# One encoder layer on one core: the weight ring moves to the upper end of the memory, and the moving operands of scores, up and down projection to its lower half

## The chip, the core and the metric

The kernel runs on one core of a Trainium2 chip. The metric is the time of one execution in microseconds of device time. Of the engines that the texts name, TensorE (PE in the profile) multiplies matrices, VectorE (DVE) and ScalarE (ACT) work elementwise, GpSimd (POOL) does little here, and SyncE (SP) issues the transfers. A matmul holds a 128x128 block still in the array (the stationary operand) and passes the other one through (the moving operand, 128, 256 or 512 columns here).

## What is computed

```python
u  = rmsnorm(x, norm1_g)
hq, hi, hf_f, hf_b, hgate, aq, ak, av, ga, gb = split(u @ w_in)
o_a = hgrn2_bidirectional(hq, hi, hf_f, hf_b, hgate, ...)   # gated linear recurrence, 4 heads
o_b = gqa_bidirectional(aq, ak, av, ...)                    # rotary attention, 8 heads on 2 kv heads
merged = sigmoid(ga) * (o_a @ w_branch_a) + sigmoid(gb) * (o_b @ w_branch_b)
x  = x + merged @ w_out
up = dwconv_centred(rmsnorm(x, norm2_g) @ w_up, conv_w, conv_b)
val, gate = split(up)
x  = x + (silu(gate) * val) @ w_down
```

All arrays are fp32; x is 1024 x 1024, w_in 1024 x 5376 in ten parts, w_up 1024 x 5632, w_down 2816 x 1024.

## The kernel before

Every fp32 operand of a large product is split into a high part (a cast to fp32r on ACT, L77) and a low part (the difference, on DVE, L78), and every product is three matmuls: high by high, high by low, low by high (`mm3`, L91 to L94; `gate_steps`, L276; `product`, L761). A list `name_h`, `name_l`, or one tile with both halves, holds the two parts.

The stages follow one another on PE, with work of the next stage mixed in by a scheduler of the framework, which sets the order of instructions on each engine from the program and from priorities (`tc.high_priority`):

- The first norm and transposition of x into `uT` (four tiles of 16 KiB a partition), and the products `vg`, `hp`, `v`, `sg` of the recurrence, with the recurrence itself. In `hp` and in the gate products `gp` (L276) `uT` moves, 512 columns at a time; in `v`, `sg` and later `rk`, `rq` (`gemm_t`) `uT` is stationary and 256 columns of weight move.
- Attention: `scores` (L567, L568) with `qT` stationary and `kT` moving, 512 columns; `turn` transposes the probabilities; `values` (L598) with `vv` stationary and the transposed probabilities moving, 256 columns. Gate products fill the gaps (`fill`).
- The two branch products `y` (weights stationary, branch outputs `oah`, `oal`, `ob`, `obh`, `obl` moving) and `wo` (`mT` stationary, the split w_out moving).
- The up projection as seven products (`m1` to `m7`) for each of 22 blocks j. Weight blocks are stationary; the moving operands are `c0b` and `c1t` (in the pool `cp`) and `xt3`, `xt4`, `xb22` (in the pool `xr`), all 512 columns. `hidden` applies the convolution and the gate and writes the left operands of the down projection to `left_d`.
- The down projection as seven products of eleven steps each (`down`). A step n = 0, 1, 2, ... loads a left block (`left`), splits it and a block of w_down (or a sum of two) into `dz`, and does twelve matmuls into four banks: four of L92, then pairs of L93 and L94. In the first product the banks are called `da`.

Memory is handed out by pools. Pools without `side` are put one above the other from the bottom of a partition, those with `side="right"` one below the other from the top, and each keeps its place until it is closed. The offsets in this text are bytes of a partition, counted up from the pools' sizes. Before, `const` ends at 19,584; `wpool` (the ring `wp` of three 8-KiB slots, and two `raw` buffers of 4 KiB) lies at 19,584 to 52,352; `uT`, and after it the tiles of `cp`, at 52,352 to 117,888; then the small gate buffers. At the right, `kT` and `vv`, later `ob0`, `ob1`, `wo00`, `wo02`, `wo03`, lie at 172,000 to 196,576 (`apk`), and `xt3`, `xt4`, `xb22` between 133,088 and 182,240 (`xr`). `dz` is a tile of the ring.

The loads of w_down into the blocks `W[0][k]` (L968) and of the left blocks (L979) go through SP's queue, as do the stores of `hidden` into `left_d` (L898, L907). Before, the blocks of w_down have places in `c0w` (8 halves), `c1w` (16 halves) and ten tiles `w`; left blocks 0 to 7 have places in `c0left`, 8 to 10 in `raw` buffers, and from step 11 on they come through a ring of four tiles `dr`. L1024 is a difference of two blocks of w_down, which a later product needs.

Of the kernel before, what the change touches and what calls it, by code (L numbers as in the profile page):

```python
# [17 lines left out]
P = 128  # L18
# [26 lines left out]
def hybrid_kernel(ctx: ExitStack, tc: tile.TileContext, x, gn, vec, cst, rope,  # L45
# [10 lines left out]
    wpool = pool("wpool", 2, wst)  # L56
# [85 lines left out]
    mid = ExitStack()  # L142
    upool = pool("upool", 1, mid)
    uT = [tuple(upool.tile([P, KT, 512], F32R, name=f"uT{i}{n}") for n in "hl") for i in range(2)]

    gstp = pool("gstp", 2, mid)
# [29 lines left out]
    def gate_silu(sg, u):  # L176
        for i in range(2):
# [16 lines left out]
          [wide(np_.tile([P, 2 * L], F32R, name=f"vg1{n}", bufs=1)) for n in "hl"]]  # L194

    def wide_block(i, n):
        raw = wpool.tile([P, L], F32, tag="raw", name=f"raw_vg{i}{n}")
        nc.sync.dma_start(raw, win_t[2 * n + i])
        split(vg[i][0][:, :, n, :], vg[i][1][:, :, n, :], raw.rearrange("p (k c) -> p k c", k=4))

    def wide_gemm(t):
        ps = gps.tile([P, 512], F32, tag="g", name=f"vg_{t}")
        h, l = uT[t // 4]
        o = slice((t % 4) * P, (t % 4 + 1) * P)
        for k in range(KT):
            bh, bl = (z[:, k % 4].rearrange("p n c -> p (n c)") for z in vg[k // 4])
            end = mm3(ps, h[:, k, o], l[:, k, o], bh, bl, k == 0, k == KT - 1)
        S.copy(vts[0][:, t, :], ps[:, 0:256])
        V.tensor_copy(sg[:, t, :], ps[:, 256:512])
        return end  # L210
# [57 lines left out]
    def gate_steps(c):  # L268
        wh, wl = weight_block(win_f[12 + c], f"g{c}")
        for half in range(2):  # L270
            ps = gps.tile([P, 512], F32, tag="g", name=f"gp{c}{half}")
            h, l = uT[half]
            for k in range(KT):
                w = slice(k * P, (k + 1) * P)
                for n, (a, b) in enumerate(((wh, h), (wh, l), (wl, h))):
                    yield T.matmul(ps, a[:, w], b[:, k, :], start=k == 0 and n == 0, stop=k == KT - 1 and n == 2)  # L276
            gt = gstp.tile([P, 512], F32, tag="gt", name=f"gt{c}{half}")
            S.copy(gt, ps)
            nc.sync.dma_start(gate_d[c, :, half * 512:(half + 1) * 512], gt)
# [159 lines left out]
    apk = pool("apk", 1, kst, side="right")  # L439
# [187 lines left out]
    mid.close()  # L627


    cst_ = ExitStack()  # L630
    cp = pool("cp", 2, cst_)
    xs2 = lambda t: cp.tile([P, D], F32, tag="xs", name=f"xs2{t}", bufs=1)
    cols = lambda tag, name: tuple(cp.tile([P, KT, 512], F32R, tag=tag, name=f"{name}{n}") for n in "hl")
# [78 lines left out]
    def normed_columns(t):  # L712
        nc.sync.dma_start(h_d[t], acc[t])
        xs = normed(xs2(t), acc[t], gb2, f"b{t}")
# [62 lines left out]
    def prep_sums(j):  # L777
        r1 = r1s.pop(j)
        r2 = cp.tile([P, 2, NH], F32, tag="xs", name=f"r2_{j}", bufs=1) if j else two(slot_v("r2_0", F32)[0])
# [42 lines left out]
    a22 = cp.tile([P, 2, NH], F32, tag="xs", name="a22_0", bufs=1)[:, 1]  # L822
# [20 lines left out]

    xr = pool("xr", 1, ust, side="right")
    xr_tile = lambda tag, j, shape, dt=F32, n=1: xr.tile(shape, dt, tag=tag, name=f"{tag}_{j}", bufs=n)
    split_4(0, a22)
    for nm in ("t3", "t4", "b22"):
        xop[nm] = tuple(xr.tile([P, 4, NH], F32R, name=f"x{nm}{n}") for n in "hl")
# [106 lines left out]
    wq, early = eight("c0w"), eight("c0left")  # L955
    early = [early[:, i] for i in range(KT)]
    for i in range(2):
        r = wpool.tile([P, 2, NH], F32, tag="raw", name=f"left{i}")
        early += [r[:, 0], r[:, 1]]
    where = [wq[:, 2 * i:2 * i + 2] for i in range(4)]  # L960
    for wq in (eight("c1w0"), eight("c1w1")):
        where += [wq[:, 2 * i:2 * i + 2] for i in range(4)]
    where += [dl_.tile([P, 2, NH], F32, tag="w", name=f"w{i}", bufs=10) for i in range(10)]
# [8 lines left out]
    def down(ps, i, first, right, load=None, after=None):  # L972

        for k in range(NK):
            n = next(nstep)
            raw = dl_.tile([P, 2, NH], F32, tag="raw", name=f"dr{n}", bufs=4) if n >= NK else None
# [5 lines left out]
            z = [y.rearrange("p (n c) -> p n c", n=2) for y in halves(ring(f"dz{n}"))]  # L982
# [154 lines left out]
```

## Time and profile before

| | before |
|---|---|
| time, median of 3 runs (lowest to highest) | 1601.61 us (1598.26 to 1604.12) |
| profiled execution: its own time | 1601.28 us |
| profiled execution: span, first to last instruction | 1599.2 us |
| mean granted TensorE clock | 0.997 |
| PE busy | 1567.0 us (98%), 8056 matmuls |
| weight loads (PEld) busy, beside PE | 1309.5 us (82%) |
| DVE busy | 1113.4 us (70%) |
| ACT busy | 771.0 us (48%) |
| POOL busy | 35.1 us (2%) |

The span is 2.1 us shorter than the profiled execution's own time. Busy times are sums over all instructions of an engine. Matmuls are pipelined: one that is listed with 0.39 us starts some 0.23 us after the one ahead of it, so the distance of two starts, and not the duration, is what a matmul takes of PE's time.

### The profile page before, as it was taken

What the parts mean: (1) busy time and instruction counts of PE and PEld (TensorE: products, weight loads), DVE (VectorE), ACT (ScalarE), POOL (GpSimd) and SP (SyncE); (2) the same over time, 40 slices, a digit from 0 to 9 for tenths busy, and PEclk for the clock granted to TensorE, in tenths of its full rate; (3) what the DMA queues carried; (4) which work ended last, traced back from release to release, by engine and by line L of the source; (5) the groups of instructions that cost most, each with busy time, mean ns of one, the idle gap of its engine ahead of it and who ended that gap; (6) DMA issues with size and microseconds to landing.
All of it is one profiled execution on the core that took longest, in us unless ns stands there. A gap on an engine that the chain in (4) does not pass through costs nothing.

```text
span 1599.2 us, 20536 instructions
## 1 busy us (share of the span) xinstructions
PE 1567.0 (98%) x8056; PEld 1309.5 (82%) x8056; DVE 1113.4 (70%) x1648; ACT 771.0 (48%) x1205; POOL 35.1 (2%) x33
## 2 busy tenths in 40 slices
PE   8999999999999999999999989999999999999998
PEld 6889998889988888887888867788788788787887
DVE  5367566545768888887653387787888787967586
ACT  5276354524556566666432344444544444544432
POOL 0000000000000000000000061000000000000000
PEclk9999999999999999999999999999999999999999
DMA  5011111222010101012444112322232234685333
GB/s 205 27 40 40 53 40 53 81 77 80 27 60 27 47 32 42 27 47 106 154 151 179 57 46 66 106 102 96 99 99 99 101 111 139 223 308 185 100 119 105
DMA packets 59761, 150.29 MB, mean 94 GB/s; under 512 B 6161, under 2 KB 6417, under 8 KB 59666
## 3 DMA queue, kind: packets, MB, share of 16 engines
q1 hardware_dynamic: 59666, 148.99, 27.6%
q8 instruction: 63, 1.03, 0.3%
q14 instruction: 32, 0.26, 0.1%
HBM read 109.91 MB, written 39.06 MB: 93 GB/s over the span
## 4 chain that ended last, share of the span: by engine, by line
PE 83%; DVE 7%; DMA 4%; ACT 4%; issue 1%; SPq 1%; DVEq 0%; ACTq 0%
PE pa L761 13%; PE gp L276 10%; PE pc L761 6%; PE pt L587 4%; PE pv L598 4%; PE pb L761 3%; PE s L567 2%; PE y L92 2%; PE y L94 2%; PE y L93 2%; PE hp L93 2%; PE hp L94 2%; PE hp L92 2%; PE s L568 2%; PE wo L94 2%; PE wo L93 2%
## 5 line engine op out<-in xcount | busy, mean ns | idle before, releaser
L77 ACT CAST pth<-pt 128x512 fp32r<-128x512 f32 x128 | 71.2, 588 | 59.2 <-PE pt L587 58.9
L77 ACT CAST dz<-dr 128x512 fp32r<-128x512 f32 (+1 forms) x66 | 50.6, 767 | 101.8 <-PE da L94 35.8
L78 DVE TENSOR_TENSOR dz<-dr,dz 128x512 fp32r<-128x512 f32 (+1 forms) x66 | 56.9, 867 | 50.5 <-ACT dz L77 50.2
L573 ACT ACTIVATE p<-s,m 128x1024 f32<-128x1024 f32 x64 | 71.9, 1123 | 34.1 <-DVE m L570 34.1
L276 PE MATMUL gp<-uT1h,w_g 128*128 128x512 f32 x256 | 86.1, 397 | 0.0
L276 PE MATMUL gp<-uT0h,w_g 128*128 128x512 f32 x256 | 86.0, 396 | 0.0
L78 DVE TENSOR_TENSOR ptl<-pt,pth 128x512 fp32r<-128x512 f32 x128 | 82.4, 681 | 4.6 <-ACT pth L77 4.6
L570 DVE TENSOR_REDUCE m<-s 128x1 f32<-128x1024 f32 x64 | 78.1, 1220 | 6.2 <-PE s L568 4.4
L761 PE MATMUL pc<-c1t,wb 128*128 128x512 f32 x264 | 69.5, 398 | 5.4 <-ACT c1t L77 5.0
L761 PE MATMUL pa<-c0b,wa 128*128 128x512 f32 x264 | 69.1, 394 | 4.0 <-ACT wa L77 2.9
L587 PEld LDWEIGHTS pt<-cs,p 128*128 128x128 f32 x512 | 56.4, 140 | 19.9 <-DVE ptl L78 9.5
L587 PE MATMUL pt<-cs,p 128*128 128x128 f32 x512 | 71.0, 277 | 1.6 <-DVE p L575 0.9
L761 PE MATMUL pb<-c0b,wa 128*128 128x512 f32 x264 | 68.7, 391 | 0.5 <-DVE ta L734 0.5
L761 PE MATMUL pa<-c1t,wb 128*128 128x512 f32 x264 | 67.5, 393 | 0.0
L598 PE MATMUL pv<-pth,vv 128*128 128x256 f32 x256 | 65.2, 293 | 0.0
L77 ACT CAST wc<-r 128x1024 fp32r<-128x1024 f32 x22 | 23.1, 1052 | 86.3 <-PE pc L761 76.5
L761 PEld LDWEIGHTS pc<-c1t,wb 128*128 128x128 f32 x264 | 50.5, 192 | 17.0 <-ACT c1t L77 5.2
L761 PEld LDWEIGHTS pa<-c0b,wa 128*128 128x128 f32 x264 | 48.9, 188 | 17.5 <-ACT wa L77 5.6
L598 PE MATMUL pv<-ptl,vv 128*128 128x256 f32 x256 | 62.6, 282 | 0.4 <-DVE ptl L78 0.4
L761 PEld LDWEIGHTS pa<-c1t,wb 128*128 128x128 f32 x264 | 49.8, 189 | 12.0 <-DVE c1t L78 0.4
L761 PEld LDWEIGHTS pb<-c0b,wa 128*128 128x128 f32 x264 | 49.5, 188 | 11.5 <-DVE ta L734 0.9
L888 DVE SCALAR_TENSOR_TENSOR cv<-c,vc,cv 128x1023 f32<-128x1023 f32 x44 | 56.2, 1278 | 2.5 <-ACT cv L887 2.5
(461 smaller groups left out, 4467.4 us busy)
## 6 DMA issues: line engine op xcount, KB each, us to landing
r<-in_wup_dram SPq DMA_DIRECT2D x44, 512.0 KB, 3.4
left_d<-cv SPq DMA_DIRECT2D x33, 512.0 KB, 3.2
dr<-left_d SPq DMA_DIRECT2D x66, 256.0 KB, 2.7
raw_g<-in_win_f_dram SPq DMA_DIRECT2D x16, 512.0 KB, 3.4
gate_d<-gt SPq DMA_DIRECT2D x32, 256.0 KB, 2.0
gl<-gate_d SPq DMA_DIRECT2D x16, 512.0 KB, 4.0
raw_h<-in_win_f_dram SPq DMA_DIRECT2D x12, 512.0 KB, 3.4
w<-in_wdown_dram SPq DMA_DIRECT2D x20, 256.0 KB, 5.4
```

The source lines that it names most:

```text
L77: S.copy(h, src)
L78: V.tensor_tensor(out=l, in0=src, in1=h.bitcast(F32), op=ALU.subtract)
L92: T.matmul(ps, ah, bh, start=first, stop=False, skip_group_check=more)
L93: T.matmul(ps, ah, bl, start=False, stop=False, skip_group_check=more)
L94: return T.matmul(ps, al, bh, start=False, stop=last, skip_group_check=more)
L276: yield T.matmul(ps, a[:, w], b[:, k, :], start=k == 0 and n == 0, stop=k == KT - 1 and n == 2)
L570: V.tensor_reduce(out=m, in_=s, axis=AX.X, op=ALU.max, negate=True)
L573: S.activation(pb, s, AF.Exp, bias=m, accum_out=z)
L587: pin(T.transpose(pt[:, i, :], pb[:, k * P:(k + 1) * P], ident))
L598: pin(T.matmul(pv, vv[pair // 2][:, k, :], pts[u][k // 4][n][:, k % 4, :, :], start=k == 0 and n == 0, stop=k == KT - 1 and n == 1))
L761: T.matmul(ps, a[:, k * P:(k + 1) * P], x[:, k, :], start=first and n == 0, stop=n == len(seq) - 1, skip_group_check=not first)
L888: V.scalar_tensor_tensor(out=cv[:, 1:], in0=src[:, :-1], scalar=w0, in1=cv[:, 1:], op0=ALU.mult, op1=ALU.add)
```

## The change

The pools change places, and some tiles change pools; no product, split or transfer of the large arrays is left out. `wpool` opens on the right side and lies at 192,480 to 225,248, with one row buffer `xs` of 4 KiB above it. `cp` opens at the start, at 19,584 to 85,120, and `uT` lives in its tiles. `apk` (`kT`, `vv`, `ob0`, `ob1`, `wo00`, `wo02`, `wo03`, `r2_0`) opens on the left, at 85,120 to 109,696. `xt3`, `xt4`, `xb22` get a pool of their own on the left, `xl`, at 85,120 to 134,272 (`xb22h` from 117,888 to 126,080, `xb22l` above it). What used the gate buffers and `cp`'s tag `xs` uses the row buffer. `vg1` is split in four halves of 4 KiB, with two more casts and two more differences. In the down projection `dz` has three fixed places in `c0dz` and `c0left`; the left blocks 0 to 3 lie in the rest of `c0left`, 4 to 9 in the `raw` buffers and the row buffer, and step 10 is the first that loads through `dr`. The blocks of w_down lie in `c1w` (16 halves), in the three tiles of the ring (`w`) and in eight tiles `wd`; the early places `c0w` are gone.

```diff
-    wpool = pool("wpool", 2, wst)
+    wpool = pool("wpool", 2, wst, side="right")
...
-    mid = ExitStack()
-    upool = pool("upool", 1, mid)
-    uT = [tuple(upool.tile([P, KT, 512], F32R, name=f"uT{i}{n}") for n in "hl") for i in range(2)]
-
-    gstp = pool("gstp", 2, mid)
+
+    cst_ = ExitStack()
+    cp = pool("cp", 2, cst_)
+    row = lambda name: wpool.tile([P, D], F32, tag="xs", name=name, bufs=1)
+    cols = lambda tag, name: tuple(cp.tile([P, KT, 512], F32R, tag=tag, name=f"{name}{n}") for n in "hl")
+    uT = [cols(f"c{i}", f"uT{i}") for i in range(2)]
...
-          [wide(np_.tile([P, 2 * L], F32R, name=f"vg1{n}", bufs=1)) for n in "hl"]]
+          [[hp2.tile([P, L], F32R, tag="k", name=f"vg1{n}{i}", bufs=4).rearrange("p (k n c) -> p k n c", k=2, n=2)
+            for i in range(2)] for n in "hl"]]
...
+        gt = row(f"gt{c}")
...
-            gt = gstp.tile([P, 512], F32, tag="gt", name=f"gt{c}{half}")
-            S.copy(gt, ps)
-            nc.sync.dma_start(gate_d[c, :, half * 512:(half + 1) * 512], gt)
+            w = slice(half * 512, (half + 1) * 512)
+            S.copy(gt[:, w], ps)
+            nc.sync.dma_start(gate_d[c, :, w], gt[:, w])
...
-    apk = pool("apk", 1, kst, side="right")
+    apk = pool("apk", 1, kst)
...
-        xs = normed(xs2(t), acc[t], gb2, f"b{t}")
+        xs = normed(row(f"xs2{t}"), acc[t], gb2, f"b{t}")
...
-        r2 = cp.tile([P, 2, NH], F32, tag="xs", name=f"r2_{j}", bufs=1) if j else two(slot_v("r2_0", F32)[0])
+        r2 = two(row(f"r2_{j}")) if j else two(slot_v("r2_0", F32)[0])
...
+    xl = pool("xl", 1, ust)
     xr = pool("xr", 1, ust, side="right")
...
-        xop[nm] = tuple(xr.tile([P, 4, NH], F32R, name=f"x{nm}{n}") for n in "hl")
+        xop[nm] = tuple(xl.tile([P, 4, NH], F32R, name=f"x{nm}{n}") for n in "hl")
...
-    wq, early = eight("c0w"), eight("c0left")
-    early = [early[:, i] for i in range(KT)]
+    za, zb = cp.tile([P, 2, 2, L], F32R, tag="c0", name="c0dz"), cp.tile([P, 2, 2, L], F32R, tag="c0", name="c0left")
+    dz = [za[:, 0], za[:, 1], zb[:, 0]]
+    early = [zb[:, 1, i // 2, (i % 2) * NH:(i % 2 + 1) * NH].bitcast(F32) for i in range(4)]
     for i in range(2):
-        r = wpool.tile([P, 2, NH], F32, tag="raw", name=f"left{i}")
+        r = two(wpool.tile([P, L], F32, tag="raw", name=f"left{i}"))
         early += [r[:, 0], r[:, 1]]
-    where = [wq[:, 2 * i:2 * i + 2] for i in range(4)]
+    r = two(row("left2"))
+    early += [r[:, 0], r[:, 1]]
+    where = []
...
-    where += [dl_.tile([P, 2, NH], F32, tag="w", name=f"w{i}", bufs=10) for i in range(10)]
+    for i in range(3):
+        wq = ring(f"w{i}", F32)
+        where += [two(wq[:, n]) for n in range(2)]
+    where += [dl_.tile([P, 2, NH], F32, tag="w", name=f"wd{i}", bufs=8) for i in range(8)]
...
-            raw = dl_.tile([P, 2, NH], F32, tag="raw", name=f"dr{n}", bufs=4) if n >= NK else None
+            raw = dl_.tile([P, 2, NH], F32, tag="raw", name=f"dr{n}", bufs=4) if n >= len(early) else None
...
-            z = [y.rearrange("p (n c) -> p n c", n=2) for y in halves(ring(f"dz{n}"))]
+            z = [y.rearrange("p (n c) -> p n c", n=2) for y in halves(dz[n % 3])]
```

The order of instructions changes most where the up projection ends and the down projection begins. The line numbers of the changed kernel are up to eleven higher there: L878, L886, L893, L894, L909, L917, L918, L920, L921, L990 and L1035 answer to L873, L881, L888, L889, L904, L912, L913, L915, L916, L979 and L1024.

On DVE before, around the splits of step 2 of the down projection (`dz_11649`; `dz_11668` is step 3):

```order
L78 TENSOR_TENSOR dz_11649<-c0left,dz_11649 128x512
L1024 TENSOR_TENSOR c1w_11598<-c1w_11598 128x512
L889 SCALAR_TENSOR_TENSOR cv_11491<-c_10_11324,vc,cv_11491 128x1023
L78 TENSOR_TENSOR dz_11649<-c0w,dz_11649 128x512
L1024 TENSOR_TENSOR c1w_11597<-c1w_11597 128x512 x3
L915 TENSOR_TENSOR cv_11355<-cv_11355,cv_11224 128x512
L888 SCALAR_TENSOR_TENSOR cv_11567<-c_21_11539,vc,cv_11567 128x1023
L904 TENSOR_TENSOR cv_11487<-cv_11487,cv_11491 128x1024
L881 TENSOR_TENSOR c_21_11456<-pc_11512,u_21_11510 128x512
L78 TENSOR_TENSOR dz_11668<-c0left,dz_11668 128x512
L916 TENSOR_TENSOR cv_11355<-cv_11355 128x512
L78 TENSOR_TENSOR dz_11668<-c0w,dz_11668 128x512
```

On DVE in the changed kernel, around the splits of step 2, whose place is `c0left` (rows that write `c0dz` from a left or W block are steps 3 and 4):

```order
L1035 TENSOR_TENSOR w_11587<-w_11587 128x512
L1035 TENSOR_TENSOR c1w_11584<-c1w_11584 128x512
L909 TENSOR_TENSOR cv_11472<-cv_11472,cv_11476 128x1024
L1035 TENSOR_TENSOR c1w_11585<-c1w_11585 128x512 x3
L886 TENSOR_TENSOR c_21_11441<-pc_11497,u_21_11495 128x512
L1035 TENSOR_TENSOR c1w_11585<-c1w_11585 128x512
L1035 TENSOR_TENSOR c1w_11584<-c1w_11584 128x512
L78 TENSOR_TENSOR c0dz<-left_11581,c0dz 128x512
L1035 TENSOR_TENSOR c1w_11584<-c1w_11584 128x512
L78 TENSOR_TENSOR c0left<-c1w_11584,c0left 128x512
L1035 TENSOR_TENSOR c1w_11584<-c1w_11584 128x512
L78 TENSOR_TENSOR c0dz<-c1w_11585,c0dz 128x512
```

Step 2's left block is now split much earlier (ahead of this piece), but the split of its block of w_down (the row `c0left<-c1w_11584`) stands behind the sum `c_21`, which needs the last product of the up projection, and behind the differences L1035, which before stood on `c0w` further up.

On ACT before, the casts of steps 9 to 11 of the down projection (`dz_11807`, `dz_11844`, `dz_11866`; `left_11596` is step 10's left block):

```order
L77 CAST dz_11787<-c1w_11598 128x512
L77 CAST dz_11807<-left_11596 128x512
L77 CAST dz_11807<-c1w_11598 128x512
L77 CAST dz_11844<-c1w_11598 128x512
L77 CAST dz_11844<-dr_11840 128x512
L77 CAST dz_11866<-w_11599 128x512
L77 CAST dz_11866<-dr_11862 128x512
```

On ACT in the changed kernel, the casts of steps 9 to 12 (`left_11583` holds the left blocks of steps 8 and 9, `dr_11782` the left block of step 10):

```order
L77 CAST c0dz<-left_11583 128x512
L77 CAST c0dz<-w_11586 128x512
L77 CAST c0dz<-w_11587 128x512
L77 CAST c0left<-w_11587 128x512
L77 CAST c0dz<-w_11588 128x512
L77 CAST c0dz<-dr_11782 128x512
L77 CAST c0left<-dr_11818 128x512
```

The cast of step 10's left block now stands behind the casts of W blocks of steps 11 and 12, of which that of step 12 writes the place of `c0dz` that step 9 read.

On SP before, the queue around step 10's left block (`left_11596`) and the first `dr`:

```order
L907 DMA left_d_79<-cv_11487 128x512
L898 DMA left_d_78<-cv_11355 128x2x512
L979 DMA left_11596<-left_d_79 128x512
L898 DMA left_d_79<-cv_11567 128x2x512
L898 DMA left_d_79<-cv_11487 128x2x512
L898 DMA left_d_79<-cv_11567 128x2x512
L979 DMA dr_11840<-left_d_69 128x512
L968 DMA w_11599<-in_wdown_dram 128x512 x2
```

On SP in the changed kernel, the same stretch; `dr_11782` is step 10's left block:

```order
L912 DMA left_d_79<-cv_11472 128x512
L979 DMA w_11588<-in_wdown_dram 128x512 x4
L903 DMA left_d_78<-cv_11340 128x2x512
L903 DMA left_d_79<-cv_11552 128x2x512
L903 DMA left_d_79<-cv_11472 128x2x512
L903 DMA left_d_79<-cv_11552 128x2x512
L990 DMA dr_11782<-left_d_79 128x512
L979 DMA wd_11589<-in_wdown_dram 128x512 x2
L990 DMA dr_11818<-left_d_69 128x512
```

The load for step 10 moved from ahead of the last three stores of `hidden` to behind them.

## Rows read from the trace of the kernel before

**Rows 1.** Busy time by stretch: the attention and the up projection.

```profile
450.00:765.00 315.00, 308.13 (x1811) 256.74 (x1810) 252.27 (x409) 193.76 (x371) 0.00 (x0) 0.99 0.14 49
...
950.00:1386.00 436.00, 426.07 (x1832) 343.24 (x1831) 356.34 (x412) 205.26 (x257) 13.18 (x6) 0.99 0.33 112
```

**Rows 2.** Timeline of PE (start, us, instruction): branch product, 36 matmuls between these starts.

```profile
802.66 0.40 PE L92 MATMUL y<-obh,w_ab 128*128 128x512 f32 x1
...
811.06 0.40 PE L92 MATMUL y<-oah,w_ab 128*128 128x512 f32 x1
```

**Rows 3.** Timeline of PE: steps 7 and 10 of the down projection, 36 matmuls apart.

```profile
1402.08 1.07 PE L92 MATMUL da<-dz 128*128 128x512 f32 x4
...
1410.24 1.07 PE L92 MATMUL da<-dz 128*128 128x512 f32 x4
```

**Rows 4.** Timeline of PE: the last 11 gate matmuls before the k projection, then 12 of 256 columns.

```profile
365.75 0.39 PE L276 MATMUL gp<-uT1l,w_g 128*128 128x512 f32 x1
...
368.26 0.28 PE L92 MATMUL rk<-w_kv,uT0h 128*128 128x256 f32 x1
...
369.69 0.28 PE L92 MATMUL rk<-w_kv,uT0h 128*128 128x256 f32 x1
```

**Rows 5.** Timeline of PE: four score matmuls, and 13 of attention's values, between these starts.

```profile
642.14 0.40 PE L567 MATMUL s<-kT,qT 128*128 128x512 f32 x1
...
643.07 1.21 PE L587 MATMUL pt<-cs,p 128*128 128x128 f32 x8
...
644.36 0.28 PE L598 MATMUL pv<-pth,vv 128*128 128x256 f32 x1
...
645.91 0.28 PE L598 MATMUL pv<-ptl,vv 128*128 128x256 f32 x1
```

**Rows 6.** Timeline of PE in the up projection: runs of one product each.

```profile
981.17 1.09 PE L761 MATMUL pa<-xt4h,w4h 128*128 128x512 f32 x4
...
983.94 2.03 PE L761 MATMUL pc<-xb22h,wc 128*128 128x512 f32 x8
...
987.21 2.02 PE L761 MATMUL pa<-xt3h,wc 128*128 128x512 f32 x8
...
990.01 1.09 PE L761 MATMUL pa<-c0b,wa 128*128 128x512 f32 x4
...
1366.00 2.92 PE L761 MATMUL pa<-c1t,wb 128*128 128x512 f32 x12
1368.76 1.98 PE L761 MATMUL pc<-c1t,wb 128*128 128x512 f32 x8
```

**Rows 7.** Busy time of 10 us at the end of the up projection.

```profile
1380.00:1390.00 10.00, 10.00 (x45) 8.12 (x44) 10.00 (x15) 5.40 (x8) 0.00 (x0) 1.00 0.54 208
```

**Rows 8.** Timeline of DVE there.

```profile
1388.25 1.22 DVE L904 TENSOR_TENSOR cv<-cv,cv 128x1024 f32<-128x1024 f32 x1
1389.39 0.68 DVE L881 TENSOR_TENSOR c<-pc,u 128x512 f32<-128x512 f32 x1
1389.99 0.68 DVE L78 TENSOR_TENSOR dz<-c0left,dz 128x512 fp32r<-128x512 f32 x1
...
1407.58 0.69 DVE L916 TENSOR_TENSOR cv<-cv 128x512 f32<-128x512 f32 x1
```

**Rows 9.** Timeline of PE there; the bracket is the wait before and its releaser.

```profile
1387.29 1.08 PE L92 MATMUL da<-dz 128*128 128x512 f32 x4
...
1391.93 0.50 PE L93 MATMUL da<-dz 128*128 128x512 f32 x1 [0.84 <-DVE dz L78]
```

**Rows 10.** Timeline of SP's queue there: the last three stores of `hidden`.

```profile
1403.25 5.42 SPq L898 DMA_DIRECT2D left_d<-cv  x3
```

**Rows 11.** Timeline of ACT: the first cast of a block from `dr`.

```profile
1412.17 0.62 ACT L77 CAST dz<-dr 128x512 fp32r<-128x512 f32 x1 [3.83 <-DMA dr<-left_d]
```

**Rows 12.** Timeline of PE at the start.

```profile
22.70 0.50 PE L92 MATMUL vg<-vg0h,uT0h 128*128 128x512 f32 x1 [0.62 <-ACT uT0h L77]
```

**Rows 13.** DMA issues of the page: KB each, median us to landing.

```profile
dr<-left_d SPq DMA_DIRECT2D x66, 256.0 KB, 2.7
```

More of the change, by code (lines that the diff above doesn't have):

```diff
@@ L198, in wide_block @@
         nc.sync.dma_start(raw, win_t[2 * n + i])
-        split(vg[i][0][:, :, n, :], vg[i][1][:, :, n, :], raw.rearrange("p (k c) -> p k c", k=4))
+        raw = raw.rearrange("p (k c) -> p k c", k=4)
+        if i == 0:
+            split(vg[0][0][:, :, n, :], vg[0][1][:, :, n, :], raw)
+        else:
+            for b in range(2):
+                split(vg[1][0][b][:, :, n, :], vg[1][1][b][:, :, n, :], raw[:, 2 * b:2 * b + 2])
     def wide_gemm(t):
@@ L205, in wide_gemm @@
         for k in range(KT):
-            bh, bl = (z[:, k % 4].rearrange("p n c -> p (n c)") for z in vg[k // 4])
+            bh, bl = ((z[:, k] if k < 4 else z[k // 2 - 2][:, k % 2]).rearrange("p n c -> p (n c)")
+                      for z in vg[k // 4])
             end = mm3(ps, h[:, k, o], l[:, k, o], bh, bl, k == 0, k == KT - 1)
@@ L626, in hybrid_kernel @@
     at.close()
[L627 to L633, printed above, removed]
     yst = ExitStack()
@@ L821, in hybrid_kernel @@
     prep_sums(0)
-    a22 = cp.tile([P, 2, NH], F32, tag="xs", name="a22_0", bufs=1)[:, 1]
+    a22 = two(row("a22_0"))[:, 1]
     nc.sync.dma_start(a22, wup[0, :, NH:])
```

## The prediction

> **What bounds the kernel now.** I read the busy time by stretch first, then PE's timeline inside the stretches, then the engines around the end of the up projection. The stretches show PE as the bound nearly everywhere: 426.07 of 436 us in the up projection and 308.13 of 315 us in attention, while DVE has 356.34 and 252.27 there [rows 1]. So a change pays where it shortens the distance between two matmuls, or lengthens a wait of PE, and hardly elsewhere. The timeline is then to be read for distances of starts, with the moving operand's place beside each.
>
> Matmuls of 512 columns come in two distances. In the branch products, whose moving operands lie above 125,000, 36 matmuls take 8.40 us, 233.3 ns each [rows 2]. In the down projection, where the moving `dz` lies below 44,160, 36 take 8.16 us, 226.7 ns [rows 3]. Gate matmuls with `uT` moving (52,352 to 117,888) take 2.51 us for eleven, 228.2 ns [rows 4]. Scores, both operands high, take 0.93 us for four, 232.5 ns [rows 5]. Inside one stage, the up projection, with the same stationary ring throughout: twelve of `xt3` take 2.80 us (233.3 ns), twelve of `xb22` and two of `c1t` 3.27 us (233.6), twelve of `xt4` 2.77 us (230.8), and twelve of `c1t`, which lies low, 2.76 us (230.0) [rows 6]. A moving operand in the upper part thus goes with some 5 ns more, less clearly in `xt4`. The stationary operand's place does not show: scores with it high are no slower than `xt3` with it low. At 256 columns nothing shows: twelve `rk` (moving low) take 1.43 us, thirteen `pv` (moving high) 1.55 us, 119.2 ns both [rows 4, 5].
>
> By the Trainium skill, "SBUF — State Buffer", section "Who interferes with whom", PE has one read port for the moving operand and an independent one for weight loads and never waits on another engine; nothing there makes an address dear, so by this page the moves alone would be worth nothing. The rows disagree by 6.6 ns of 226.7, and I go by the rows, but keep that reading as a rival.
>
> **The change, part by part.** The sum is made against the profiled execution, 1601.28 us, which is the median of the runs shown (1601.61) within 0.33 us; its span is 1599.2, and the 2.1 us outside stay.
>
> *Up projection.* `xt3`, `xt4` and half or more of `xb22` go low. There are 22 blocks with twelve matmuls of each, 264. As their new distance I take 229 ns, between the gates' 228.2 and `c1t`'s 230.0. `xt3`: 264 x 4.3 = 1.1 us. `xt4`: 264 x 1.8 = 0.5. `xb22`: 4.6 ns on 132, since its high half lies at 117,888 to 126,080, and no row says where between 117,888 and 125,000 the step is: 0.6. Together -2.2 us; with all of `xb22` and the 226.7 of the down projection it would be 264 x (6.6 + 4.1 + 6.9) = -4.6.
>
> *Scores.* 32 units x 2 heads x 4 = 256 matmuls from 232.5 to 228.2: -1.1. PE idles 6.9 us in this stretch, so some of it turns into waiting: -0.8.
>
> *Branch and output products.* `ob0` and `ob1` are two of eight moving pairs of `y`, 96 of 384 matmuls; `wo00`, `wo02`, `wo03` are three of eight blocks of `wo`, 144 of 384, and up to 56 more whose tiles the change slides to the middle. I have read `wo` as going at `y`'s distance. At 5.1 ns: -0.5 and -0.9. The four together are -4.4 us, with bounds of -3 (1.5 ns less for each of 900 matmuls) and -8 (226.7 ns as the new distance).
>
> *Start.* The two extra casts and differences are of half size, so the same bytes are split; they end earlier for the first half. PE waits 0.62 us there for a cast [rows 12], of which I count half: -0.3, with bounds of -0.6 and, if the extra instructions come late, +0.6.
>
> *One row buffer instead of two gate buffers.* A gate half is 24 matmuls x 228.2 ns = 5.5 us, and a 256-KB transfer lands 2.7 us after its issue [rows 13], so the buffer's half is read long before the next gate's copy. Nothing; if PE ran ahead of the copies, at most those 2.7 us once.
>
> *Moves that I cost at nothing.* With the ring high, 3428 matmuls of 512 columns have moving low and stationary high (gates 768, `hp` 576, scores 256, `y` 112, up projection 1716). No row shows that pair. Its bounds are the fastest and the slowest row, 1.5 ns below the gates' and 5.1 ns above; I take no change, since scores with a high stationary lie below `xt3`. The 960 matmuls of 256 columns (`v`, `sg`, `rk`, `rq`) get a high moving operand under a low stationary one: nothing by `pv`, or 5.1 ns if the step of 512 columns came back, +4.9 us.
>
> *From up to down projection.* Here the change costs. DVE is busy for all of 1380 to 1390 [rows 7], so its order decides. Step 2's W split stood before `c_21` and now stands behind it and four rows more. `c_21` needs the up projection's last product. In the changed order four matmuls stand between that and step 2, which PE reached at 1387.29 [rows 9], so the product ends near 1387.29 - 0.9 = 1386.4. DVE then needs 0.60 us for each of `c_21`, three differences and a split (0.60 is the distance of two starts, 1389.39 to 1389.99), and 0.68 for the split itself: 3.7 us, so at the earliest 1390.1 [rows 8]. PE does step 2's four L92 matmuls, needing only the high part, until 1388.2, then waits: 1.9 us at least. If DVE gets to `c_21` no sooner than before (1389.39), it is 4.9. I take 2.4, near the lower end, as the cast of the left block is moved ahead and two long operations behind. The 0.84 us that PE waits at 1391.93 goes [rows 9], as step 3 is split earlier now. Net +1.5 (+1.1 to +4.1).
>
> Late next is step 10. It comes at 1410.24 [rows 3] + 1.5 = 1411.7. ACT must first cast step 12's W into the place that step 9 has just left, 0.62 us, and then the left block, 0.62 [rows 11]: PE waits 1.2 us. The load itself is now behind the three stores that end issuing at 1408.67 [rows 10], which wait for DVE's last difference at 1407.58 [rows 8]; with 2.7 us to land it is there at 1411.4, just hidden, and if DVE's delay of 1.5 carried through it would be 1.2 us late, in the same wait. So +1.2 (0 to +2). The transition is +2.7 us (+1.1 to +6.1).
>
> **Sum.** -4.4 - 0.3 + 2.7 = -2.0 us: 1601.28 - 2.0 = **1599.3 us**.
>
> **The rivals.**
>
> 1. *The transition is hidden.* DVE has caught up by the time of step 2, and the stalls shrink to 0.5 us, while the new distance is nearer 226.7: -5.5 + 0.5 gives 1596.3; at the far bound, -8.3, it is 1593. For it: DVE's total work does not grow. Against it: DVE is full just there [rows 7], and `c_21` cannot come before PE's product.
>
> 2. *Places count for nothing.* The distances belong to the stages (which queues and writes run beside), not to addresses. Then only the transition and the start remain: 1601.3 + 2.7 - 0.3 = 1603.7. Against it: the two distances stand side by side in one stage under one stationary ring [rows 6]. For it: `xt4` is hardly slower than `c1t`. This is what the page of the skill named above would give.
>
> 3. *A high weight ring costs* (the other side). If a stationary operand from above delays a matmul whose moving one comes from below, all 3428 pay. From 2.0 ns each it makes the kernel more than 0.3% slower (3428 x 2.0 = 6.9 us, less the 2.0); at the full 5.1 ns it is +17.5 us, 1616.8. For it: the pair does not occur before. Against it: scores [rows 5].
>
> 4. *The 256-column matmuls pay the step*: +4.9 us, 1604.2. Against it: `pv` [rows 5].
>
> **How the numbers follow.** The forecast case (gains as counted, both stalls) has 0.47, rival 1 0.27, rival 2 0.10, rival 3 0.07, rival 4 0.09. About 0.3%, 4.8 us, is what a measurement of this kernel can tell from no change. The forecast, rivals 2 and 4 lie within it. Faster by more is rival 1, and an edge of the forecast: 0.30. Slower by more is rival 3, and a transition at its upper bound together with rival 4: 0.10. Within: 0.60. Leaving out rival 3 and the far end of rival 1 (0.05), and a little of the worst transition, the range is 1594.5 to 1605. The forecast alone, gains of 3 to 6 and a transition of 1 to 5, spans 1596 to 1603.
>
> **What would show it.** Right: twelve `xt3` in 2.75 us instead of 2.80; four scores in 0.91 to 0.92; `y` unchanged except `ob0`, `ob1`; `gp`, `pb` as before; `pv`, `rk` at 119 ns; PE waiting about 2.4 us on DVE in step 2 of `da`, no 0.84 at step 3, and about 1.2 us on ACT in step 10. Wrong: gate matmuls above 230 ns (rival 3), `rk` above 122 (rival 4), `xt3` still at 233 (rival 2), or no wait over 1 us between 1380 and 1415 (rival 1). A new stall far from these places would break the sum itself.

## The result and the profile after

The changed kernel takes 1611.84 us (median of five runs, 1610.74 to 1615.45), the kernel before 1601.93 us beside it (1598.26 to 1604.12): a ratio of 1.0068, 95% interval 1.0050 to 1.0087. It is 10 us slower; the forecast was 2 us faster, with a range that ended at 1605. The profiled execution has a span of 1611.4 us against 1599.2, at a granted clock of 0.996 against 0.997. The rows below come from these two executions, which are 12.2 us apart.

The timeline of PE in the changed kernel, at the places that answer to [rows 2], [rows 4], [rows 5] and [rows 6]: the last eleven gate matmuls before `rk`, four scores, 36 of `y`, and runs of `xt3`, `xt4` and `c1t` in the up projection.

```profile
368.92 0.40 PE L285 MATMUL gp<-uT1l,w_g 128*128 128x512 f32 x1
...
371.49 0.28 PE L92 MATMUL rk<-w_kv,uT0h 128*128 128x256 f32 x1
...
372.92 0.29 PE L92 MATMUL rk<-w_kv,uT0h 128*128 128x256 f32 x1
...
646.03 0.39 PE L576 MATMUL s<-kT,qT 128*128 128x512 f32 x1
...
646.96 1.17 PE L596 MATMUL pt<-cs,p 128*128 128x128 f32 x8
...
805.83 0.39 PE L92 MATMUL y<-oah,w_ab 128*128 128x512 f32 x1
...
814.09 0.40 PE L92 MATMUL y<-ob,w_ab 128*128 128x512 f32 x1
...
987.84 2.04 PE L765 MATMUL pa<-xt3h,wc 128*128 128x512 f32 x8
...
990.66 1.10 PE L765 MATMUL pa<-c0b,wa 128*128 128x512 f32 x4
...
995.81 1.10 PE L765 MATMUL pa<-xt4h,w4h 128*128 128x512 f32 x4
...
998.62 1.57 PE L765 MATMUL pa<-c1t,wb 128*128 128x512 f32 x6
...
1372.63 2.98 PE L765 MATMUL pa<-c1t,wb 128*128 128x512 f32 x12
1375.44 2.03 PE L765 MATMUL pc<-c1t,wb 128*128 128x512 f32 x8
```

Read the distances of starts again. Gates went from 228.2 ns to 2.57 us / 11 = 233.6. `c1t` went from 230.0 to 2.81 / 12 = 234.2, although its own place stayed low: what moved up is the ring that holds its stationary operand. `xt3` stayed slow, 2.82 / 12 = 235.0 against 233.3, and `xt4` went from 230.8 to 234.2, though both now lie low. Scores stayed at 0.93 / 4 = 232.5. And `y`, three quarters of whose moving operands still lie high, became faster: 8.26 / 36 = 229.4 against 233.3. At 256 columns `rk` has 1.43 us for twelve, 119.2 ns, as before, now with its moving operand high.

The recurrence's projections `hp` show it best, 36 matmuls between these starts. Before:

```profile
84.71 0.39 PE L92 MATMUL hp<-uT1h,w_h 128*128 128x512 f32 x1
...
92.87 0.39 PE L92 MATMUL hp<-uT0h,w_h 128*128 128x512 f32 x1
```

After:

```profile
85.12 0.40 PE L92 MATMUL hp<-uT1h,w_h 128*128 128x512 f32 x1
...
93.56 0.40 PE L92 MATMUL hp<-uT0h,w_h 128*128 128x512 f32 x1
```

8.16 us became 8.44: 226.7 to 234.4 ns, with the same moving operand, low in both kernels.

The lost time can be followed by events that both timelines have. The first `rk` comes 3.2 us later (371.49 against 368.26). At the first `xt3` run shown it is 0.6 (987.84 against 987.21): the branch products and the start of the up projection gave most of that back. At the last `c1t` run it is 6.6 (1372.63 against 1366.00): 6.0 us were lost inside the up projection. The other 5.6 us of the 12.2 come behind that, most of them where the down projection begins, in PE's timeline after:

```profile
1395.41 1.19 PE L92 MATMUL da<-c0left 128*128 128x512 f32 x4 [1.25 <-ACT c0left L77]
1398.10 0.65 PE L93 MATMUL da<-c0left 128*128 128x512 f32 x1 [1.50 <-DVE c0left L78]
...
1422.27 0.50 PE L92 MATMUL da<-c0dz 128*128 128x512 f32 x1 [1.43 <-ACT c0dz L77]
...
1425.77 0.50 PE L92 MATMUL dc<-c0left 128*128 128x512 f32 x1 [0.49 <-ACT c0left L77]
```

These are steps 2, 10 and 11: 4.67 us of waits, where before there was one of 0.84 [rows 9], 3.8 us more. Another 1.6 us go behind the two waits of step 2. The row of that stretch (us; busy time and number on PE, PEld, DVE, ACT, POOL; granted clock, DMA share, GB/s):

```profile
1398.00:1401.50 3.50, 3.40 (x8) 2.67 (x9) 3.50 (x6) 0.31 (x2) 0.00 (x0) 0.54 0.79 293
```

Eight matmuls take 3.4 us, which at 227 ns each would take 1.8. The granted clock is 0.54 there: for most of the stretch TensorE ran at 1.2 GHz instead of 2.4, right after it had waited 1.25 and 1.50 us.

What the first three waits are for stands in the timelines of ACT and DVE:

```profile
1393.74 0.58 ACT L882 COPY c<-pa 128x512 f32<-128x512 f32 x1 [3.49 <-PE pa L765]
1394.22 0.62 ACT L77 CAST c0dz<-left 128x512 fp32r<-128x512 f32 x1
1394.74 0.62 ACT L77 CAST c0left<-c1w 128x512 fp32r<-128x512 f32 x1
...
1420.87 0.62 ACT L77 CAST c0dz<-w 128x512 fp32r<-128x512 f32 x1 [2.10 <-PE da L94]
1421.60 0.62 ACT L77 CAST c0dz<-dr 128x512 fp32r<-128x512 f32 x1
```

```profile
1394.36 0.68 DVE L886 TENSOR_TENSOR c<-pc,u 128x512 f32<-128x512 f32 x1
1394.96 1.28 DVE L1035 TENSOR_TENSOR c1w<-c1w 128x512 f32<-128x512 f32 x2
1396.16 0.68 DVE L78 TENSOR_TENSOR c0dz<-left,c0dz 128x512 fp32r<-128x512 f32 x1
1396.76 0.68 DVE L1035 TENSOR_TENSOR c1w<-c1w 128x512 f32<-128x512 f32 x1
1397.36 0.68 DVE L78 TENSOR_TENSOR c0left<-c1w,c0left 128x512 fp32r<-128x512 f32 x1
```

On ACT the cast of step 2's W stands behind a copy that itself waits 3.49 us for an up product; on DVE its difference is the fifth row, counted from `c_21`. In step 10 the cast of step 12's W waits for PE to leave step 9, and the cast of step 10's left block comes behind it, 0.73 us after its start (1421.60 less 1420.87). Casts that wait for nothing start 0.52 us apart (1394.22, 1394.74), so the left block held its cast up a little too, as a later kernel shows.

### The profile page after: what moved, and what is told of

Its sections match the earlier page's. It is cut to its first block, busy times and chain, and to the rows that moved or that the text cites. A ratio compares the mean times of both kernels' runs of the same rounds, so it can differ in the third digit from the quotient of the medians.

```text
span 1611.4 us, 20587 instructions
## 1 busy us (share of the span) xinstructions
PE 1575.7 (98%) x8056; PEld 1312.9 (81%) x8056; DVE 1113.0 (69%) x1650; ACT 770.3 (48%) x1207; POOL 35.1 (2%) x33
## 4 chain that ended last, share of the span: by engine, by line
PE 85%; DVE 7%; ACT 3%; DMA 3%; issue 1%; SPq 0%; DVEq 0%; ACTq 0%
PE pa L765 13%; PE gp L285 10%; PE pc L765 6%; PE pv L607 4%; PE pt L596 3%; PE pb L765 3%; PE hp L93 2%; PE hp L94 2%; PE s L576 2%; PE hp L92 2%; PE y L93 2%; PE y L94 2%; PE y L92 2%; PE s L577 2%; PE da L93 2%; PE wo L94 2%
## 5 line engine op out<-in xcount | busy, mean ns | idle before, releaser
L77 ACT CAST c0dz<-dr 128x512 fp32r<-128x512 f32 (+1 forms) x45 | 34.5, 767 | 65.8 <-PE dd L93 14.0
L78 DVE TENSOR_TENSOR c0dz<-dr,c0dz 128x512 fp32r<-128x512 f32 (+1 forms) x45 | 38.9, 867 | 32.5 <-ACT c0dz L77 30.2
L765 PEld LDWEIGHTS pa<-c1t,wb 128*128 128x128 f32 x264 | 49.8, 189 | 12.2
L893 DVE SCALAR_TENSOR_TENSOR cv<-c,vc,cv 128x1023 f32<-128x1023 f32 x44 | 56.3, 1279 | 3.0 <-ACT cv L892 2.9
```

The lines of the kernel that those rows point to most:

```text
L77: S.copy(h, src)
L78: V.tensor_tensor(out=l, in0=src, in1=h.bitcast(F32), op=ALU.subtract)
L765: T.matmul(ps, a[:, k * P:(k + 1) * P], x[:, k, :], start=first and n == 0, stop=n == len(seq) - 1, skip_group_check=not first)
L893: V.scalar_tensor_tensor(out=cv[:, 1:], in0=src[:, :-1], scalar=w0, in1=cv[:, 1:], op0=ALU.mult, op1=ALU.add)
```

## The experiments

Three theories were open after this. **Parts of the memory**: a matmul is slow when its two operands lie in different parts, low and high. **The ring**: a high stationary operand costs by itself. **The stages**: places do not count, and the distances come from what runs beside. The first four kernels were to tell them apart, and to take the wait at the down projection out and put it in alone. Each ratio is to executions of the kernel before that ran beside it (medians 1601.36, 1601.33 and 1600.88 us).

**A map of places.** A kernel that computes nothing of the layer: matmuls over one large tile, each of N = 11 places of the moving operand (23 to 211 KiB up a partition) with each of 11 of the stationary one (27 to 215 KiB), REP = 24 matmuls of 512 columns a pair; then some pairs with 256 and 128 columns.

```diff
+    for i in range(N):
+        for j in range(N):
+            run(i, j, 512, REP)
```

> A kernel that computes nothing of the layer: matmuls of fp32r data from x, 24 in a row for each of 11 places of the moving operand and 11 places of the stationary one, spread over a partition from 23 KiB to 219 KiB, first with 512 moving columns (all 121 pairs), then 256 and 128 (16 pairs each). Its time is not compared; the distance of starts is. Theory 1 (what counts is whether both operands lie in the same part of the memory): about 227 ns for both low, about 234 for one low and one high whichever it is, and both high at 227 to 231. Rival 2 (each operand that lies high costs by itself): moving high 234 with any stationary, stationary high 234 with any moving, both high 234 or more. Rival 3 (places count for nothing, the distances belong to the stages): one distance within 1 ns for all pairs. At 256 and 128 columns theory 1 expects no difference or one below 1 ns.

Its busy time in one stretch (us; busy time and number on PE, PEld, ACT, POOL; granted clock, DMA share, GB/s), which holds pairs of many places, near and far; the other stretches read alike.

```profile
100.00:200.00 100.00, 100.00 (x443) 82.81 (x442) 0.00 (x0) 0.00 (x0) 1.00 0.00 1
```

Besides one or two that reach over an edge, 100 us hold 441 matmuls, 226.7 ns each. All pairs had that distance but the one with which the kernel starts (the first run is slower in all three kernels of this kind and is left out). So rival 3 of this expectation came out, and neither the parts nor the ring's height can be the cause as such.

**The ring low again**, in the changed kernel.

```diff
-    wpool = pool("wpool", 2, wst, side="right")
+    wpool = pool("wpool", 2, wst)
```

> The changed kernel with the ring, the raw buffers and the row buffer opened on the left again; the other pools slide up by 36 KiB, so that most moving operands of gates, recurrence projections and the cp products stay in the lower part beside the ring. Theory 1 and rival 2: gates 768 x 4.6 ns, projections 576 x 6.5 and up products with cp operands 1056 x 5.7 come back, 3.5 + 3.7 + 6.0 = 13 us, less 1 to 2 us that the branch products gained by both operands high: 1599 to 1601 against 1611 to 1612, with the wait of 5 to 6 us at the start of the down projection still there. Rival 3: 1611 as before this edit, since stages and order are the same.

1601.62 us, ratio 1.0008 (0.9998 to 1.0017), just above the 1599 to 1601 expected: the ring's place is worth the 10 us, with the rest of the program unchanged. That speaks against the stages as firmly as the map speaks against the places. One run of `xt3` in PE's timeline:

```profile
985.18 1.98 PE L765 MATMUL pa<-xt3h,wc 128*128 128x512 f32 x8
...
987.90 1.07 PE L765 MATMUL pa<-c0b,wa 128*128 128x512 f32 x4
```

Twelve in 2.72 us, 226.7 ns, against 233.3 before and 235.0 in the changed kernel: with the ring left low, the gain that was forecast for `xt3` comes. PE's waits at the down projection are still there (1.24, 1.66, 1.23 and 0.52 us), so the gains of the moves and the cost of the transition are about level in this kernel.

**The down projection's places as before**, in the changed kernel (`dz` in the ring, now high; `c0w`, `c0left`, ten `w`).

> The changed kernel with the down projection's places as before (dz in the ring, which is now high; c0w, c0left, ten w tiles). The da stretch took 6 us more in the changed kernel. If that is the order at the transition, it goes: minus 5 to 6 us. The 924 down matmuls then have both operands high: theory 1 expects 0 to 3 ns each, 0 to 3 us, so 1606 to 1609; rival 2 expects at least 6.5 ns each, 6 us, so 1611 to 1613.

1608.84 us, ratio 1.0047 (1.0032 to 1.0062), 3.0 us below the changed kernel by the medians and 5.1 by the profiled spans (1606.3 against 1611.4); 1606 to 1609 was expected if parts counted. PE's timeline has one wait at the start of `da`, as before, and then the steps:

```profile
1398.31 0.50 PE L93 MATMUL da<-dz 128*128 128x512 f32 x1 [0.79 <-DVE dz L78]
...
1403.01 1.07 PE L92 MATMUL da<-dz 128*128 128x512 f32 x4
...
1411.17 1.07 PE L92 MATMUL da<-dz 128*128 128x512 f32 x4
```

36 matmuls take 8.16 us, 226.7 ns each, exactly as in [rows 3], with both operands high. So a high ring as such costs nothing where the moving operand lies in it too.

**The down projection's new places alone**, in the kernel before.

> The kernel before with only the down projection's new places (dz in c0dz and c0left, W blocks in c1w, ring and wd). All operands of the down projection stay low as before. If the transition is what costs 5 to 6 us: 1606 to 1608 against 1601 to 1602, with PE waiting for DVE in step 2 of da and for ACT in step 10, as the prediction placed them. If the transition's wait comes from the ring's place or the earlier order, this kernel is within 1 us of the one before.

1607.83 us, ratio 1.0045 (1.0028 to 1.0062), as expected (1606 to 1608). PE's timeline has the waits of steps 2 and 10, and ACT's has what the last of them waits for:

```profile
1388.96 1.19 PE L92 MATMUL da<-c0left 128*128 128x512 f32 x4 [1.25 <-ACT c0left L77]
1391.56 0.50 PE L93 MATMUL da<-c0left 128*128 128x512 f32 x1 [1.41 <-DVE c0left L78]
...
1414.56 0.50 PE L92 MATMUL da<-c0dz 128*128 128x512 f32 x1 [1.86 <-ACT c0dz L77]
```

```profile
1413.88 0.62 ACT L77 CAST c0dz<-dr 128x512 fp32r<-128x512 f32 x1 [0.54 <-DMA dr<-left_d]
```

So in step 10 the load of the left block lands last, behind ACT's order. 4.52 us of waits less the 0.84 of before are 3.7 us, which is what the profiled span grew (1602.9 against 1599.2); the medians lie 6.5 apart, 4.5 to 10 by the interval. The profiled execution is the fastest of four, at a mean granted clock of 0.996. The others have 1607.46 us at 0.995, 1608.20 at 0.994 and 1609.98 at 0.993. Stretches at the lower clock, like the one in the changed kernel's profile, would account for that, but no trace of these three shows it, and in the profiled one the same two waits were not followed by one. The transition is a cost of its own: 3.7 us by the profile, 4.5 or more by the medians.

**Phases.** What the map had in common everywhere was that all operands began a multiple of 1024 bytes apart. In the two kernels the left pools begin at 19,584, which is 128 modulo 256, and the right ones at places that are 224 modulo 256 (192,480, 172,000, 133,088); modulo 64 they are 0 and 32. So I took the distance modulo 64 as the new theory. A second kernel that computes nothing begins its runs m elements (of 4 bytes) into a moving tile and s into a stationary one:

```diff
+OFFS = (0, 1, 2, 4, 8, 16, 24, 32)
...
+    for m in OFFS:
+        for s in OFFS:
+            run(m, s, 512, REP)
```

> A kernel that computes nothing of the layer: two tiles of fp32r data, one moving and one stationary, and runs of 24 matmuls that begin 0, 4, 8, 16, 32, 64, 96 or 128 bytes into each tile, all 64 pairs at 512 columns, and 0, 32, 64 bytes at 256 and 128 columns. The first map, in which all operands began at multiples of 64 bytes, had one distance everywhere, 226.7 ns, so the parts of the memory are out. New theory (phase): what counts is the place of the two operands in 64 bytes; in the two kernels the right-hand pools begin 32 bytes off the left-hand ones. It expects 226.7 where both begin at the same place modulo 64 (0 with 64 and 128, 32 with 96), 233 to 235 where one is 32 off the other, and something between, or as slow, for 4, 8 and 16. Rival (something of the stages that goes with the pools): 226.7 throughout.

```profile
36.64 5.76 PE L39 MATMUL zerowide<-mov,sta 128*128 128x512 f32 x24
42.24 5.77 PE L39 MATMUL keeperwide<-mov,sta 128*128 128x512 f32 x24
47.85 5.76 PE L39 MATMUL zerowide<-mov,sta 128*128 128x512 f32 x24
53.45 5.86 PE L39 MATMUL moverwide<-mov,sta 128*128 128x512 f32 x24
```

The first three rows have the moving operand at 0 and the stationary one 64, 96 and 128 bytes further: 5.60 us / 24 = 233.3 ns each. So a distance does slow matmuls with nothing else running, but 64 and 128 do it as well as 32: the modulus 64 was wrong. Pairs that began 32, 64, 96 or 128 bytes into both tiles, which themselves lie 17 x 256 bytes apart, took 227 to 228; those that began 4, 8 or 16 bytes into both took 231 to 233. Below 32 bytes the distance alone does not decide: moving 16 bytes in with stationary 4 or 32 bytes in took 227.

**A pad of 32 bytes on the right**, for both kernels, and one of 64 as a control. They ran beside the phases, when the modulus was still taken as 64.

```diff
     const = pool("const", 1)
+    pool("pad", 1, side="right").tile([P, 8], F32, name="pad")
```

> The kernel before with one unused tile of 32 bytes a partition opened first on the right, so that all right-hand tiles slide down by 32 bytes; nothing else changes. Of the 512-column matmuls 1344 had the moving operand 32 bytes off and the stationary one not; now 48 have. Phase: 1296 x 6.2 ns = 8 us less, perhaps 1 us more from the 520 that had both 32 off: 1591 to 1594 against 1601. Rival: no change.

> The changed kernel with the same tile of 32 bytes. Of its 512-column matmuls 3544 have the stationary operand alone 32 off and 288 the moving one alone; now 48 are left. Phase: 3784 x 6.2 ns = 23 us less, of which some may turn into waits of PE for DVE and ACT: 1588 to 1594 against 1611.8, that is, level with or a little above the kernel before with the pad, from which it then differs only by the wait of some 4 us at the down projection and by the start. Rival: no change, 1611.

> Control: the kernel before with an unused tile of 64 bytes on the right instead. All right-hand tiles slide down by 64 bytes and keep their place modulo 64. Phase: as the kernel before, 1601 within 1.5 us. If sliding itself, or the unused tile, did something, it would show here as with 32 bytes.

The kernel before: 1596.69 us, ratio 0.9970 (0.9958 to 0.9982), half of what was expected. The changed kernel: 1604.85, 1.0023 (1.0012 to 1.0035), 7 us faster than without, a third of it. The control: 1599.05, 0.9992 (0.9982 to 1.0001), 2.3 below the kernel before by the medians where 1.5 was allowed. So 32 bytes of unused memory change the time, and 64 hardly do; but not by what modulo 64 would give.

**Distances modulo 256.** One more kernel that computes nothing: runs of 48, a bank `same` for multiples of 256 bytes between the operands, `other` for the rest. Six pairs of runs at other places come first (`other` 128 bytes off), then the distances:

```diff
+DIFFS = (32, 64, 96, 128, 160, 192, 224, -32, -64, -96, -128, -192)
...
+    for d in DIFFS:
+        run(other, max(d, 0), max(-d, 0))
+        run(same, 0, 0)
```

> A kernel that computes nothing of the layer: runs of 48 matmuls of 512 columns that write a bank called same, where moving and stationary operand begin a multiple of 256 bytes apart, and a bank called other, where they do not: first six pairs of runs with the operands at other places, the others always 128 bytes off; then distances of +32, 64, 96, 128, 160, 192, 224, -32, -64, -96, -128, -192 bytes (moving less stationary), each followed by a run of same. Theory (phase in 256 bytes): each same 48 x 226.7 ns = 10.88 us, wherever its operands are; each other 48 x 233 to 234 = 11.2 us, with +64 and -192 (the same distance in 256) at 229 to 230, 11.0 us. Rival (phase in 64 bytes): +64, 128, 192 at 10.88 like same.

```profile
31.19 11.06 PE L37 MATMUL same<-mov,sta 128*128 128x512 f32 x48
42.08 11.31 PE L37 MATMUL other<-mov,sta 128*128 128x512 f32 x48
53.23 11.06 PE L37 MATMUL same<-mov,sta 128*128 128x512 f32 x48
...
97.30 11.06 PE L37 MATMUL same<-mov,sta 128*128 128x512 f32 x48
108.19 11.31 PE L37 MATMUL other<-mov,sta 128*128 128x512 f32 x48
...
163.46 11.17 PE L37 MATMUL other<-mov,sta 128*128 128x512 f32 x48
174.47 11.09 PE L37 MATMUL same<-mov,sta 128*128 128x512 f32 x48
185.40 11.38 PE L37 MATMUL other<-mov,sta 128*128 128x512 f32 x48
196.61 11.08 PE L37 MATMUL same<-mov,sta 128*128 128x512 f32 x48
```

By starts, `same` takes 10.89 us (42.08 less 31.19; the moving operand begins 256 bytes into its tile there), 226.9 ns a matmul, and the same with both operands 32 bytes into their tiles (108.19 less 97.30). `other` takes 11.15 at 128 bytes off (53.23 less 42.08), 232.3; at +64 bytes 11.01, 229.4; at +96 11.21, 233.5. The runs further on (+128 to -192) have 10.99 at -192, which is +64 again modulo 256, and 11.16 to 11.24 at all others. This is as the theory had it, to about 1 ns.

The pads of 32 and 64 bytes fit this table too. In the kernel before, 32 bytes put the high moving operands at +64 from the low ring, and twelve `xt3` took 2.75 us there (229.2 ns); 64 bytes put them at +32, 2.79 us (232.5). In the changed kernel 32 bytes leave them at -64 from the high ring, 2.80 us (233.3).

**A pad of 96 bytes on the right**, which puts both sides at 128 modulo 256: for the kernel before, the changed kernel, and the changed kernel with the down projection's places as before.

```diff
+    pool("pad", 1, side="right").tile([P, 24], F32, name="pad")
```

> The kernel before with one unused tile of 96 bytes on the right: all large tiles of both sides then begin at the same place in 256 bytes (48 matmuls of wo excepted), order and all else as before. Phase in 256 bytes: 1356 matmuls from 233.7 to 227.5 and 424 from 232.2 to 228 give 8.4 + 1.8 = 10 us, some of it lost to waits for DVE: 1592 to 1595 against 1601.3, and 2 to 4 below the kernel with 32 bytes of pad. Phase in 64 bytes: as with 32 bytes of pad, 1596.7.

> The changed kernel with the same tile of 96 bytes. Phase in 256 bytes: 3343 matmuls from 234.1 to 227.8 and 261 from 233.9 give 21 + 1.6 = 22.7 us, some of it lost to waits: 1589 to 1596 against 1611.8, about 4 above the kernel before with 96 bytes, for the waits at the start of the down projection. Phase in 64 bytes: as with 32 bytes of pad, 1604.9.

> The changed kernel with the down projection's places as before and the tile of 96 bytes: without the waits at the transition and with all phases equal. If waits and phases are all that differs between the two kernels: level with the kernel before with 96 bytes, within 2 us.

The kernel before: 1591.53 us, ratio 0.9941 (0.9928 to 0.9953), half a us below what was expected. The changed kernel: 1596.41, 0.9970 (0.9958 to 0.9982), 15.4 below the same kernel without the pad. That is at the upper edge of what was expected (1589 to 1596) and 4.9 above the kernel before with the pad, where about 4 was expected; its waits at the down projection are 1.94, 2.18, 1.41 and 0.31 us in the profile, which shows the slowest of its six executions (1600.45 us, clock 0.993). The third: 1590.04, 0.9933 (0.9920 to 0.9947), level with the first as expected, with one wait of 1.89 us left there. In PE's timeline of the kernel before with 96 bytes the up projection has one distance:

```profile
976.22 1.07 PE L762 MATMUL pa<-xt4h,w4h 128*128 128x512 f32 x4
...
978.94 1.98 PE L762 MATMUL pc<-xb22h,wc 128*128 128x512 f32 x8
...
981.66 0.61 PE L762 MATMUL pc<-c1t,wb 128*128 128x512 f32 x2
982.12 1.98 PE L762 MATMUL pa<-xt3h,wc 128*128 128x512 f32 x8
...
984.84 1.07 PE L762 MATMUL pa<-c0b,wa 128*128 128x512 f32 x4
```

`xt4` 2.72 us for twelve, `xb22` 2.72, `xt3` 2.72: 226.7 ns, where [rows 6] had 230.8 to 233.6. `xt3` and `xb22` lie as high there as in the kernel before, save 96 bytes.

## Why the prediction was wrong

**What bounds the kernel, and reading by distances of starts: right.** Every part of the loss that the rows show is a longer distance of matmuls, eight of them at the lower clock, or a wait of PE.

**The two distances: right as rows, wrong as a cause.** 227 to 229 and 233 are there, and they go with places. I read them as "a moving operand in the upper part costs 5 ns, the stationary one's place does not show". The phases and the pads show that what counts is the distance of the two operands' places modulo 256. In the kernel before the ring was low (128), so a high moving operand (224) was just the one that stood off its stationary one; high went with slow without causing it. The row that should have stopped me was `xt4`, 230.8 against the 233.3 of `xt3`, both high: its stationary `w4` was high too. I noted it as less clear and moved on.

**The failed step: "Moves that I cost at nothing".** The text took "no change" for the 3428 matmuls with moving low and stationary high, "since scores with a high stationary lie below `xt3`". This is the pair of 128 and 224, and it costs as much as the other way round. `hp` alone lost 576 x 7.7 ns = 4.4 us, gates 768 x 5.4 = 4.1, and of the up products the 1056 with `c0b` and `c1t`, which had been fast, at `c1t`'s 4.2 another 4.4: 13 us by these rows. Not all of it reached the end: from the first `hp` matmul to the end of attention, where the first `y` comes 3.95 us later than before (753.75 against 749.80), 4.8 us were lost where the first two terms give 8.5; PE had idle time there that could take some (1.38 us of the 230 from 70 us on before, 0.20 after). The kernel with the ring alone back low is 10 us faster. That was rival 3, at 0.07; its size was given as up to 5.1 ns, and its sign was right. Its mechanism, a price of height, fell too: with the down projection's places as before, `dz` is moving and stationary operand at once, high in both, at 226.7 ns.

**The gains: those of the up projection and of the scores did not come.** Scores moved from two high operands to a low and a high one, 232.5 either way. `xt3` and `xb22` only exchanged which side was off. `y` did gain 3.9 ns, not by the part that moved low but because its weights came up to where its moving operands are. Of the -4.4 us the rows leave 384 x 3.9 ns = -1.5 us, from `y`, and `xt4` turned to 264 x 3.4 = +0.9. `wo`, which has no row here, gained about the 0.9 counted: its first matmul comes 1.25 us later than before (844.51 against 843.26) and its last 0.26; why was not followed. The sum also had a slip in `xb22`: the high half moves in eight of the twelve matmuls (the x8 of [rows 6]), 176 and not 132, which is 0.2 us and leaves the 3428 short by 44. With the ring left low the forecast of the up projection holds: that kernel is 1.8 us ahead of the kernel before at the first run of `xt3` (971.48 against 973.32) and 4.2 at the last (1370.79 against 1375.02), a gain of 2.4 us where 2.2 were counted.

**The start: right in sign, too small.** At the first `hp` matmul the changed kernel is 0.8 us ahead (61.05 against 61.87); -0.3 was counted, with -0.6 as the bound. What made the rest was not followed.

**256 columns at nothing: right.** 119.2 ns for `rk` with a moving operand 96 bytes off; rival 4 fell.

**The transition: right, a little small.** Foreseen were a wait of 2.4 us in step 2, the old 0.84 gone, and 1.2 in step 10. Measured were 1.25 + 1.50, none at step 3, and 1.43; 0.49 at step 11 was not foreseen, nor that ACT has a share in step 2: I had looked at DVE's order alone there, while ACT's cast of the W block stood behind a copy that waits for PE. The load of step 10's left block was taken as just hidden; with the new places alone it came 0.54 us after ACT was free for it. The sum had +2.7 us; the waits make 3.8, and the lower clock behind step 2, which the sum did not have, 1.6 more: 5.4. That this is inside the bounds of 1.1 to 6.1 is luck, as the clock was not among their reasons.

**Rival 2, that places count for nothing**, fell too, but the map comes close to it: between places a multiple of 256 bytes apart nothing counts. By the Trainium skill, "SBUF — State Buffer", section "Who interferes with whom", PE's read ports for moving operand and weights are independent. The kernel that computes nothing has no other engine at work, and its distances still depend on both places together, 226.9 against 233.5 ns: as far as addresses go, the runs do not agree with that.

**Open.** Equal places are not always enough: before, scores had both operands at 224 modulo 256 and took 232.5 ns, while `dz` in the ring of the changed kernel, at 224 too, took 226.7, and `y`, three quarters of it at 224, 229.4. With everything at 128 the fast distance holds in all the up projection's products of the rows shown. Nor is it 224 alone: `xt4` and its `w4` share one place in the kernel before, with every pad, and twelve took 2.77 us at 224 (no pad), 2.76 at 192 (32 bytes), 2.75 at 160 (64 bytes) and 2.72 at 128 (96 bytes), while `same` above was fast at the places tried with no other engine at work. Whether other engines' accesses make the difference was not tried. Why the distance +64 costs less than -64 stays open as well.

## What to carry to other kernels

Where PE is the bound and two groups of the same matmul differ by a few ns, write down the places of both operands modulo 256 before looking for another cause: an unused tile of 96 bytes made the kernel before 9 us faster, and changed nothing but the places of the tiles on the right. An attribute that goes with a cost in every row (high, low) is not yet its cause as long as a combination is missing from the rows; with 3428 matmuls on a combination that no row shows, a small kernel that measures it is worth more than the sum of the rest. When a step's data passes through two engines, read the order of both. And behind a wait of PE, read the distances of the matmuls that follow: here eight of them ran at about half the clock.

## What was not expected of the hardware

At 512 columns of fp32r, alone on the chip's core at a granted clock of 1.00 in the stretches shown, the distance of matmuls depends on where the stationary and the moving operand begin relative to each other: 226.9 ns at multiples of 256 bytes, 229.4 at +64 (moving less stationary), 232 to 234 at the other multiples of 32 tried. How far apart they are otherwise did not matter, from 4 to 192 KiB at multiples of 1024 bytes. At 256 columns the real matmuls took 119.2 ns at 0 and at 96 bytes off.
